# Weight splits queued three halves ahead of their products instead of four

## The chip, the cores and the metric

One core of a Trainium2 chip runs the whole program in one launch. The metric is the device time of that core in microseconds (us), the median of several executions. TensorE multiplies, VectorE and GpSimd do element by element work, ScalarE does functions and casts, and SyncE's queue issues most transfers. In the profile's rows PE is TensorE, PEld its loading of the stationary operand, DVE VectorE, ACT ScalarE, POOL GpSimd, SP SyncE.

## What is computed

One layer with 512 tokens and width 2048, float32. The weights of the modulation, of the two projections and of the feed-forward part are matrices of 2048 rows or columns; every matrix is read once.

```python
mod = silu(c) @ w_ada + b_ada                       # 2048 x 12288, six vectors
sh1, sc1, gt1, sh2, sc2, gt2 = split(mod, 6)
h = rms_norm(x, norm1_g) * (1 + sc1) + sh1
proj = h @ w_in
att = sparse_attention(q, k, v, iq, ik, iw)         # 8 heads, top 128 keys by an index score
rwkv = rwkv7_time_mix(y, ...)                       # 16 heads of 64, a state per head, scanned over tokens
x = x + gt1 * (concat(att, rwkv) @ w_out)
h2 = rms_norm(x, norm2_g) * (1 + sc2) + sh2
ffn = (silu(h2 @ w_gate) * (h2 @ w_up)) @ w_down    # width 5632
out = x + gt2 * ffn
```

## The kernel before

**Products.** Every large product is made of three products of a faster number format, fp32r. A weight tile `wraw` is split into a high part `whi`, a cast on ScalarE, and a low part `wlo` = `wraw` - `whi`, a subtraction on VectorE (or on GpSimd, for odd halves of the middle part of the program). The activations are split alike (`hhi`, `hlo`). TensorE adds `hhi whi`, `hlo whi` and `hhi wlo`. All operations go through one helper, so nearly every row of the profile has its line, L127, and rows are told apart by the names of the tiles.

**The weight stream.** A job is a chunk of weights, mostly 4 k-tiles of 256 columns (512 KB), with the 24 products that use it. `issue_to` loads it into one of three raw buffers. `split_to` splits it in two halves of 512 columns a partition, each with 12 products; there are four buffers for `whi` and four for `wlo`. `run_jobs` writes the stream: at the start of job i it issues the loads up to job i + 2 and splits up to a certain half, and in the middle of the job it splits one half more. `s0` is the number of a job's first half. `split_to(n)` writes the halves below n. Until now the start of a job writes its fourth half counted from `s0` (number `s0 + 3`), the middle writes number `s0 + 4`: each split stands in the queues right behind the products of the half that used its buffer last.

**What sets the order.** The program is written in one pass, and each engine runs its queue in the order in which it was written. Beside the stream, generators write the side work: the preparation of the eight RWKV pairs (`prep`), the scan, the index scores, the attention heads, the sums of the modulation (`ada_stream`, tiles `wad`, added up on GpSimd). `drive` gives each a turn after every three products. A generator goes on when a rough clock for each queue, kept while the program is written, says that its input is there (`until`) or that a queue is not too full (`room`). Splits count in that clock too, so where a split is written moves the side work.

**A preparation** runs from two small products (`pw`) through `sg` (ScalarE, then GpSimd), the scan `L` (VectorE), `kkn`, `kf`, `work` (VectorE) to the transposes `pT` on TensorE, of which the products behind them in TensorE's queue have to wait. `rr` is a reciprocal root of a norm on GpSimd, from `st` on VectorE; `hx`, `hhi`, `hlo` are the activations behind a norm.

**Stages.** Up to about 140 us the first columns of h and the low-rank products; to 600 us the rest of `w_in` beside the preparations; to 1130 us the scan, scores and heads beside the last columns; to 1345 us the out-projection; then norm 2, and gate, up and down in four parts of the width. In the feed-forward part an up-group of two tiles is closed by an evacuation that multiplies and splits on VectorE and ScalarE; there are 22.

Of the kernel before, what the change touches and what calls it, by code (L numbers as in the profile page):

```python
# [14 lines left out]
DRAM = bass.MemoryType.DRAM  # L15
# [25 lines left out]

# columns of the constant table
C_ID, C_MASK, C_CAUS, C_BLKM = 0, 128, 256, 384
# [5 lines left out]
def layer_kernel(ctx, tc, x, c, positions, w_ada, b_ada, norm1_g, w_in, q_norm_g, k_norm_g,  # L49
                 rwkv_mu, rwkv_w0, rwkv_w_up, rwkv_a0, rwkv_a_up, rwkv_g_up, rwkv_k_k, rwkv_k_a,  # L50
                 rwkv_r_k, rwkv_lnx_g, rwkv_lnx_b, w_out, norm2_g, w_ffn_gate, w_ffn_up,
                 w_ffn_down, cst_in, out, dbg=None):
    nc = tc.nc
    ctx.enter_context(tc.manual_schedule())

    # A rough clock for each queue, kept while the program is written: it decides when side work joins the queues.
    clk = dict(pe=0.0, dve=0.0, act=0.0, pool=0.0, dma=0.0)
    ready = {}
    side = {"pe": 0.0}
# [78 lines left out]
    def until(*aps):  # L138
        """let the products run on until what these hold is there."""
        t = max(ready.get(nm(a), 0.0) for a in aps) + SLACK  # L140
        while now() < t:
            yield
# [5 lines left out]
    def banks(n):  # L148
        """wait for n free banks of the side pool."""
        while True:  # L150
            for k in [k for k, v in psread.items() if v is not None and v <= now()]:
                del psread[k]
            if len(psread) + n <= 4 and side["pe"] <= SIDE:
                return
            yield
# [42 lines left out]

    # ---------------------------------------------------------------- constants
    cst = const.tile([128, C_W], F32, name="cst")  # L200
# [27 lines left out]

    # ---------------------------------------------------------------- weight stream
    jobs = []  # L230
# [3 lines left out]
    def job(view, k0, nk, c0, ncols, mms, need=None, before=None, after=None, whole=False):  # L234
        """a chunk of weights, with the products that use it; its two halves are split one by one."""
        j = dict(view=view, k0=k0, nk=nk, c0=c0, n=ncols, mms=mms, need=need, before=before, after=after, i=len(jobs),
                 hi=[], lo=[], s0=len(subs), whole=whole)
        jobs.append(j)
        subs.extend([(j, u) for u in range(min(nk, 2))])
# [25 lines left out]
    def run_jobs(a, b, eng=SP, every=3):  # L265
        for i in range(a, b):
            j = jobs[i]
            while j["need"] is not None and not j["need"]():
                yield
            if j["before"] is not None:  # L270
                j["before"]()
            issue_to(i + 3, eng)
            split_to(j["s0"] + 4)
            n = 0
            half = None
            for kk, o, l, r, st, sp in j["mms"](j):
                if half is None and j["nk"] > 1 and kk >= j["nk"] // 2 and not j["whole"]:
                    half = 1
                    split_to(j["s0"] + 5)
                mm(o, l, r, st, sp)  # L280
                n += 1
                if n % every == 0:
                    yield
            if j["after"] is not None:
                j["after"]()
# [14 lines left out]
    def group_T(view, c0, mts, klist, kc, rhs, evac, pool=PG, need=None, before=None, kneed=None, add=True, chunk_done=None, apart=False):  # L300
        """out^T tiles: mts = [(column offset, M)], contracted over klist in chunks of kc."""
        box = {}
        ncols = mts[-1][0] + mts[-1][1]
        nch = len(klist) // kc

        def mms(j, ci):
            if ci == 0:
                box["ps"] = [pool("acc") for _ in mts]
            order = [(kk, i) for kk in range(kc) for i in range(len(mts))]
            if apart and ci == nch - 1:  # L310
                order.sort(key=lambda e: e[1])
            for kk, i in order:
                ki = ci * kc + kk
                hi, lo = rhs(klist[ki])
                (off, M), ps = mts[i], box["ps"][i]
                wh, wl = j["hi"][kk][:, off:off + M], j["lo"][kk][:, off:off + M]
                yield kk, ps[:M], wh, hi, ki == 0, False
                yield kk, ps[:M], wh, lo, False, False
                yield kk, ps[:M], wl, hi, False, ki == len(klist) - 1
                if apart and ki == len(klist) - 1 and i < len(mts) - 1:  # L320
                    evac(box["ps"], [i])

        def one(ci):
            job(view, klist[ci * kc], kc, c0, ncols, (lambda j, ci=ci: mms(j, ci)),
                need=(kneed(klist[ci * kc:ci * kc + kc]) if kneed else (need if ci == 0 else None)),
                before=before if ci == 0 else None,
                after=(lambda: evac(box["ps"], *([[len(mts) - 1]] if apart else []))) if ci == nch - 1 else chunk_done,
                whole=apart and ci == nch - 1)

        if not add:  # L330
            return one
        for ci in range(nch):
            one(ci)

    # ---------------------------------------------------------------- inputs
    xtok = [[hpool.tile([128, 512], F32, name="xtok", tag="h") for _ in range(4)] for _ in range(NT)]
# [16 lines left out]

    # scale and shift, some columns at a time; the loads run as far ahead as there is room
    BLOCKS = [(0, 1), (1, 1)] + [(k, 2) for k in range(2, KD, 2)]
    pieces = []
    for k1, n1 in BLOCKS:
        for kind in ("scale", "shift"):
            n = 4 // n1
# [34 lines left out]

    # rms of x, and x transposed
    ssq = SM("ssq")
# [12 lines left out]

    # vectors as columns  # L410
    v1 = const.tile([128, 128], F32, name="v1")
# [25 lines left out]
    def tables():  # L437
        """cos and signed sin of the rotary angles, features on partitions."""
        pos = G("pos", I32)
# [4 lines left out]
        for fc, sc in ((C_FQ, C_SQ), (C_FI, C_SI)):  # L444
            ang, n, t = G("ang"), G("nrot"), G("trot")
# [26 lines left out]

    # first group: the loras and two tiles of k, as the columns of h come
    first = []
# [47 lines left out]

    # ---------------------------------------------------------------- modulation, first part
    def colsum(dst, t):
        """column 32 b + c of t, summed over the partitions of a quarter, to partition c of the quarter and column b."""
        u = G("tr")
        V.transpose(u, t)
        V.tensor_reduce(dst, u.rearrange("p (b c) -> p b c", c=32), axis=mybir.AxisListType.X, op=OP.add)

    def spread(ps, parts, col=C_MOD):  # L530
        """the quarters added up: the sum of column 128 j + q to partition q and column j."""
        pv = parts.rearrange("p (j a) -> p a j", a=4)
        for a in range(4):
            mm(ps[32 * a:32 * a + 32], cst[:, col:col + 32], pv[:, a, :])
# [58 lines left out]

    # ---------------------------------------------------------------- rwkv: evacuation with token shift
    def shifted(ps, M, mcol, name):
# [33 lines left out]

    # scratch in DRAM  # L630
    pk = dram.tile([NC, 128, PAIRS, 512], F32, name="pk")
# [143 lines left out]

    # ---------------------------------------------------------------- rwkv: triangular solve, one problem per partition
    solved = set()
# [42 lines left out]

    # ---------------------------------------------------------------- rwkv: chunk scan over all heads
    mix = {}
    scanned = set()

    def scan(g):
        """the pairs of a group, chunk after chunk."""
        while g not in solved or done["prep"] < PAIRS:
# [131 lines left out]

    # ---------------------------------------------------------------- modulation, second part  # L960
    mod = {n: const.tile([128, 16], F32, name=n) for n in ("gt1", "sh2", "sc2", "gt2")}
# [58 lines left out]

    # ---------------------------------------------------------------- attention
    iwt = const.tile([128, NT, 16], F32, name="iwt")
# [142 lines left out]

    # the four query tiles of a head share three banks
    PLACE = {3: (0, 0), 2: (1, 0), 0: (1, 384), 1: (2, 0)}
# [63 lines left out]

    # ---------------------------------------------------------------- the main stream of products
    ALLK = list(range(KD))
# [38 lines left out]

    # out projection, contracted over the rwkv half first
    mT = {}
# [61 lines left out]
    for m in range(4, KD, 2):  # L1336
        group_T(wout, m * 128, TWO, KO, 4, mixed, evac_out(m), kneed=kneed, before=load_x([m, m + 1]),
                apart=m == KD - 2)
    # the column sums of the squares need every tile
    i_norm2 = len(jobs)  # L1340
# [30 lines left out]

    # feed-forward, in parts of its width
    gate = {}
# [48 lines left out]

    # gate and up together in the first group, as the columns of h2 come
    gbox, ubox = {}, {}
# [26 lines left out]

    # ---------------------------------------------------------------- go
    start(run_rb())
# [106 lines left out]
```

## Time and profile before

| | |
|---|---|
| median of 3 runs (lowest to highest) | 2810.62 us (2807.94 to 2813.64) |
| the profiled execution's span | 2808.0 us |
| TensorE busy | 2699.7 us, 96% |
| VectorE, ScalarE, GpSimd busy | 49%, 34%, 29% |
| granted TensorE clock, mean | 0.975 of full |
| the chain that ended last: TensorE, VectorE, DMA | 81%, 9%, 4% |

The span is read by stretches: the share of TensorE's busy time and the granted clock tell which of them can give anything. A wait is shown with the engine that waited, what it waited to write, and what released it. A matmul row may be a few per cent short of records.

### The profile page before, as it was taken

The numbers are of one execution on the slowest core, as the hardware profiler recorded it, in microseconds if no ns is written. First come the engines' busy times: TensorE is split into PE (matmuls) and PEld (weight loads), VectorE is DVE, ScalarE is ACT, GpSimd is POOL, SyncE is SP. The second block draws the span as 40 slices with busy tenths as digits, with TensorE's granted clock in tenths as the row PEclk, the third lists the DMA queues.
The fourth block names the chain that finished last, engine by engine and source line by source line (L and its number), as shares of the span: only waits on it lengthen the run. The fifth ranks groups of instructions, "written<-read, shape, count | busy, mean of one in ns | idle before, by whom it ended". The sixth has DMA issues, their size and how long they took to land.

```text
span 2808.0 us, 35665 instructions
## 1 busy us (share of the span) xinstructions
PE 2699.7 (96%) x13439; PEld 2131.3 (76%) x13439; DVE 1362.6 (49%) x2064; ACT 953.0 (34%) x1691; POOL 801.9 (29%) x695
## 2 busy tenths in 40 slices
PE   7998988988999999999799999999999999999999
PEld 4576766667677768788688888888888888888887
DVE  4476445588957875743743233232333323333333
ACT  3255542332333335554452222222222222222222
POOL 2057768974434566654340000000000000000000
PEclk8999999989999999999899999999999999999999
DMA  9976765355466434464253333323333333333233
GB/s 324 312 243 202 227 184 146 103 131 174 149 198 195 137 128 136 156 220 149 77 193 98 98 98 97 97 95 96 97 98 98 98 98 98 98 98 95 93 101 110
DMA packets 383580, 396.12 MB, mean 141 GB/s; under 512 B 52442, under 2 KB 332832, under 8 KB 383408
## 3 DMA queue, kind: packets, MB, share of 16 engines
q1 hardware_dynamic: 381312, 387.78, 44.5%
q0 software_dynamic: 1952, 5.81, 0.6%
q8 instruction: 105, 1.72, 0.3%
q14 instruction: 67, 0.55, 0.1%
q10 hardware_dynamic: 144, 0.26, 0.0%
HBM read 358.13 MB, written 35.65 MB: 140 GB/s over the span
## 4 chain that ended last, share of the span: by engine, by line
PE 81%; DVE 9%; DMA 4%; POOL 2%; issue 2%; ACT 1%; SPq 1%; DVEq 0%; ACTq 0%; POOLq 0%
PE acc L127 71%; DMA wraw<-in_w_in_dram 2%; PE p L127 1%; DVE X L127 1%; PE po L127 1%; DVE stmp L127 1%; PE vacc L127 1%; DVE work L127 1%; DVE wlo L127 1%; SPq L127 1%; PE adaacc L127 1%; DMA wada<-in_w_ada_dram 1%; DVE score L127 1%; PE pV L127 1%; DVE u L127 0%
## 5 line engine op out<-in xcount | busy, mean ns | idle before, releaser
L127 DVE TENSOR_TENSOR wlo<-wraw,whi 128x512 fp32r<-128x512 f32 (+2 forms) x750 | 553.2, 743 | 1111.3 <-ACT whi L127 1104.8
L127 ACT CAST whi<-wraw 128x512 fp32r<-128x512 f32 (+2 forms) x860 | 517.9, 607 | 1251.9 <-PE acc L127 1085.7
L127 PE MATMUL acc<-hhi,whi 128*128 128x512 f32 (+1 forms) x2256 | 914.4, 405 | 4.4 <-ACT hhi L127 4.0
L127 PE MATMUL acc<-hhi,wlo 128*128 128x512 f32 (+1 forms) x2256 | 887.2, 393 | 19.2 <-DVE wlo L127 15.5
L127 PE MATMUL acc<-hlo,whi 128*128 128x512 f32 (+1 forms) x2256 | 886.2, 393 | 3.6 <-DVE hlo L127 3.6
L127 PEld LDWEIGHTS acc<-hhi,whi 128*128 128x128 f32 (+1 forms) x2256 | 425.2, 188 | 128.4 <-issue 32.4
L127 PEld LDWEIGHTS acc<-hhi,wlo 128*128 128x128 f32 (+1 forms) x2256 | 426.0, 189 | 116.3 <-DVE wlo L127 19.3
L127 PEld LDWEIGHTS acc<-hlo,whi 128*128 128x128 f32 (+1 forms) x2256 | 426.3, 189 | 95.4 <-DVE hlo L127 6.4
L127 PE MATMUL acc<-act,whi 128*128 128x512 f32 x1408 | 434.8, 390 | 0.0
L127 POOL TENSOR_TENSOR wad<-wad 128x512 f32<-128x512 f32 x240 | 343.0, 1429 | 150.5 <-ACT wad L127 139.0
L127 PEld LDWEIGHTS acc<-act,whi 128*128 128x128 f32 x1408 | 263.2, 188 | 53.8
L127 PE MATMUL acc<-act,wlo 128*128 128x512 f32 x704 | 274.0, 389 | 0.0
L127 POOL TENSOR_TENSOR wlo<-wraw,whi 128x512 fp32r<-128x512 f32 (+1 forms) x110 | 157.9, 1436 | 235.4 <-ACT whi L127 223.9
L127 ACT ACTIVATE wad<-wad,cact 128x512 f32<-128x512 f32 x256 | 179.0, 719 | 14.4 <-DMA wad<-in_w_ada_dram 14.1
L127 PEld LDWEIGHTS acc<-act,wlo 128*128 128x128 f32 x704 | 132.1, 188 | 27.6
L127 PE MATMUL acc<-mhi,whi 128*128 128x512 f32 x256 | 100.5, 392 | 0.0
L127 PE MATMUL acc<-mhi,wlo 128*128 128x512 f32 x256 | 99.7, 389 | 0.0
L127 PE MATMUL acc<-mlo,whi 128*128 128x512 f32 x256 | 99.6, 389 | 0.0
L127 DVE SCALAR_TENSOR_TENSOR x<-acc,gt,x 128x512 f32<-128x512 f32 x80 | 57.3, 750 | 41.6 <-PE acc L127 41.6
L127 POOL TENSOR_TENSOR X<-X,stmp 128x504 f32<-128x504 f32 (+33 forms) x69 | 67.0, 970 | 5.4
L127 POOL TENSOR_TENSOR stmp<-X,N 128x504 f32<-128x504 f32 (+33 forms) x69 | 63.7, 923 | 4.6 <-DVE work L127 1.4
L127 PE MATMUL vacc<-whi,hhi 128*128 128x512 f32 x128 | 58.1, 454 | 0.0
(257 smaller groups left out, 2328.5 us busy)
## 6 DMA issues: line engine op xcount, KB each, us to landing
wad<-in_w_ada_dram SPq DMA_DIRECT2D x256, 256.0 KB, 4.4
wraw<-in_w_in_dram SPq DMA_DIRECT2D x108, 512.0 KB, 5.0
wraw<-in_w_ffn_down_dram SPq DMA_DIRECT2D x88, 512.0 KB, 3.4
wraw<-in_w_ffn_gate_dram SPq DMA_DIRECT2D x84, 512.0 KB, 3.5
wraw<-in_w_ffn_up_dram SPq DMA_DIRECT2D x84, 512.0 KB, 3.4
wada<-in_w_ada_dram SPq DMA_DIRECT2D x128, 256.0 KB, 6.7
wraw<-in_w_out_dram SPq DMA_DIRECT2D x32, 512.0 KB, 3.5
pk<-pack SPq DMA_DIRECT2D x16, 768.0 KB, 3.8
```

The costliest lines, as they stand in the source:

```text
L127: return f(*args, **kw)
```

## The change

The two calls of `split_to` in `run_jobs` ask for one half less. At the start of a job the half `s0 + 2` is written, in its middle the half `s0 + 3`. Buffers and loads stay as they are in number and size. All other lines of the diff take away comments and docstrings, and are left out here.

```diff
@@ -270,13 +270,13 @@
             if j["before"] is not None:
                 j["before"]()
             issue_to(i + 3, eng)
-            split_to(j["s0"] + 4)
+            split_to(j["s0"] + 3)
             n = 0
             half = None
             for kk, o, l, r, st, sp in j["mms"](j):
                 if half is None and j["nk"] > 1 and kk >= j["nk"] // 2 and not j["whole"]:
                     half = 1
-                    split_to(j["s0"] + 5)
+                    split_to(j["s0"] + 4)
                 mm(o, l, r, st, sp)
```

VectorE's queue in the second preparation, before; `tr` and `part` belong to a sum of the modulation:

```order
L127 SCALAR_TENSOR_TENSOR L<-reset,sg 128x512
L127 SCALAR_TENSOR_TENSOR kkn<-k,v_231,prb 128x512
L127 TENSOR_SCALAR kf<-at,v_231,der 128x512
L127 TENSOR_TENSOR kf<-k,kf 128x512
L127 SCALAR_TENSOR_TENSOR work<-kkn,sg 128x8x63
L127 TENSOR_SCALAR work<-kkn 128x8
L127 TENSOR_TENSOR work<-r,sg 128x8x64
L127 TENSOR_TENSOR wlo<-wraw,whi 128x512
L127 STREAM_TRANSPOSE tr<-wad 128x512
L127 TENSOR_REDUCE part_377<-tr 128x16
L127 TENSOR_TENSOR at<-at,e_2471 128x512
L127 TENSOR_TENSOR work<-kkn,at 128x8x64
```

and the same place now:

```order
L127 SCALAR_TENSOR_TENSOR L<-reset,sg 128x512
L127 SCALAR_TENSOR_TENSOR kkn<-k,v_231,prb 128x512
L127 TENSOR_SCALAR kf<-at,v_231,der 128x512
L127 TENSOR_TENSOR kf<-k,kf 128x512
L127 SCALAR_TENSOR_TENSOR work<-kkn,sg 128x8x63
L127 TENSOR_SCALAR work<-kkn 128x8
L127 TENSOR_TENSOR work<-r,sg 128x8x64
L127 TENSOR_TENSOR at<-at,e_2484 128x512
L127 TENSOR_TENSOR work<-kkn,at 128x8x64
L127 TENSOR_TENSOR work<-kf,e_2484 128x8x64
L127 SCALAR_TENSOR_TENSOR r<-r,v_231,kf 128x512
L127 TENSOR_TENSOR wlo<-wraw,whi 128x512
```

The low part that stood between `work` and `at` has moved behind `r`, and the small sum has gone ahead of `L`.

GpSimd's queue where the heads end and the out-projection is about to begin, before:

```order
L127 TENSOR_TENSOR wad<-wad 128x512 x2
L127 TENSOR_TENSOR rr<-st,cst 128x4
L127 TENSOR_SCALAR rr<-rr 128x4
L127 TENSOR_TENSOR wad<-wad 128x512
L127 TENSOR_TENSOR rr<-st,cst 128x4
L127 TENSOR_SCALAR rr<-rr 128x4
L127 TENSOR_TENSOR wlo<-wraw,whi 128x512
L127 TENSOR_TENSOR wad<-wad 128x512
```

and now:

```order
L127 TENSOR_TENSOR wlo<-wraw,whi 128x512
L127 TENSOR_TENSOR wad<-wad 128x512 x2
L127 TENSOR_TENSOR rr<-st,cst 128x4
L127 TENSOR_SCALAR rr<-rr 128x4
L127 TENSOR_TENSOR rr<-st,cst 128x4
L127 TENSOR_SCALAR rr<-rr 128x4
L127 TENSOR_TENSOR wlo<-wraw,whi 128x512
L127 TENSOR_TENSOR wad<-wad 128x512 x2
```

The two pairs of `rr` stood ahead of one low part and `wad` additions; now they stand behind fewer additions and ahead of the low part that comes one job earlier in the stream.

VectorE's queue at the start of the feed-forward part, with the numbers of the tiles, before:

```order
L127 TENSOR_TENSOR hlo_11683<-hx_11680,hhi_11682 128x512
L127 TENSOR_TENSOR wlo_11692<-wraw_11621,whi_11691 128x256
L127 TENSOR_TENSOR wlo_11696<-wraw_11621,whi_11695 128x256
L127 TENSOR_SCALAR hx_11701<-hx_11701,gp2_376,sh2_373 128x512
L127 TENSOR_TENSOR hlo_11704<-hx_11701,hhi_11703 128x512
L127 TENSOR_SCALAR hx_11708<-hx_11708,gp2_376,sh2_373 128x512
L127 TENSOR_TENSOR hlo_11711<-hx_11708,hhi_11710 128x512
L127 TENSOR_SCALAR hx_11721<-hx_11721,gp2_376,sh2_373 128x512
L127 TENSOR_TENSOR hlo_11724<-hx_11721,hhi_11723 128x512
L127 TENSOR_TENSOR wlo_11729<-wraw_11689,whi_11728 128x256
L127 TENSOR_TENSOR wlo_11741<-wraw_11689,whi_11740 128x256
```

and now:

```order
L127 TENSOR_TENSOR hlo_11773<-hx_11770,hhi_11772 128x512
L127 TENSOR_TENSOR wlo_11782<-wraw_11677,whi_11781 128x256
L127 TENSOR_TENSOR wlo_11786<-wraw_11711,whi_11785 128x256
L127 TENSOR_SCALAR hx_11791<-hx_11791,gp2_376,sh2_373 128x512
L127 TENSOR_TENSOR hlo_11794<-hx_11791,hhi_11793 128x512
L127 TENSOR_SCALAR hx_11798<-hx_11798,gp2_376,sh2_373 128x512
L127 TENSOR_TENSOR hlo_11801<-hx_11798,hhi_11800 128x512
L127 TENSOR_SCALAR hx_11811<-hx_11811,gp2_376,sh2_373 128x512
L127 TENSOR_TENSOR hlo_11814<-hx_11811,hhi_11813 128x512
L127 TENSOR_TENSOR wlo_11819<-wraw_11711,whi_11818 128x256
L127 TENSOR_TENSOR wlo_11831<-wraw_11779,whi_11830 128x256
```

Each low part has moved back by one place in the row of low parts: of the two that stand between `hlo` and the next `hx`, the first is now the second half of the chunk before (`wraw_11677` is the chunk that `wraw_11587` was), and the second half of the next chunk (`wraw_11711`, which was `wraw_11621`) stands behind the three `hx` and `hlo`.

## Rows read from the trace of the kernel before

**Rows 1.** By stretch: length, PE, PEld, DVE, ACT, POOL busy (instructions), clock, DMA share, GB/s.

```profile
300.00:400.00 100.00, 89.15 (x463) 68.82 (x462) 53.41 (x60) 45.59 (x77) 72.35 (x55) 0.93 0.72 208
1400.00:1800.00 400.00, 400.00 (x1772) 330.97 (x1771) 138.42 (x197) 123.90 (x204) 34.03 (x26) 1.00 0.35 113
```

**Rows 2.** Waits of all engines between 140 and 460 us; engine, line, releaser: total, times, longest.

```profile
POOL wlo L127 <- ACT whi L127: 88.8, 21, 25.7
...
DVE wlo L127 <- ACT whi L127: 88.0, 23, 11.8
...
ACT whi L127 <- DMA wraw<-in_w_in_dram: 60.1, 12, 8.8
...
ACT whi L127 <- PE acc L127: 26.7, 18, 4.6
...
PE pT L127 <- DVE work L127: 23.6, 5, 5.9
```

**Rows 3.** Waits between 460 and 800 us.

```profile
PE pT L127 <- DVE work L127: 12.6, 2, 7.1
...
PE acc L127 <- DVE wlo L127: 7.1, 3, 3.7
```

**Rows 4.** Waits between 1420 and 2808 us, the feed-forward part.

```profile
ACT whi L127 <- PE acc L127: 872.2, 435, 2.6
```

**Rows 5.** Timeline of VectorE and GpSimd, preparations; start, length, operation, [idle before, releaser].

```profile
211.73 0.63 POOL L127 TENSOR_SCALAR sg<-sg 128x512 f32<-128x512 f32 x1
...
212.86 1.63 DVE L127 TENSOR_TENSOR_SCAN L<-reset,sg 128x512 f32<-128x512 f32 x1
...
250.11 0.69 DVE L127 TENSOR_TENSOR wlo<-wraw,whi 128x512 fp32r<-128x512 f32 x1 [7.91 <-ACT whi L127]
...
257.33 1.77 DVE L127 TENSOR_TENSOR wlo<-wraw,whi 128x512 fp32r<-128x512 f32 x1
...
260.36 1.76 DVE L127 TENSOR_TENSOR at<-at,e 128x512 f32<-128x512 f32 x1
...
451.88 0.62 POOL L127 TENSOR_SCALAR sg<-sg 128x512 f32<-128x512 f32 x1
...
456.75 2.07 DVE L127 TENSOR_TENSOR_SCAN L<-reset,sg 128x512 f32<-128x512 f32 x1
```

**Rows 6.** Stretches behind two of the waits at pT; columns as in the first group.

```profile
226.00:232.00 6.00, 5.86 (x36) 4.49 (x36) 5.56 (x7) 3.96 (x7) 5.87 (x4) 0.74 0.75 236
573.00:579.00 6.00, 6.00 (x33) 4.47 (x31) 5.44 (x7) 0.76 (x2) 5.76 (x6) 0.64 0.08 26
```

**Rows 7.** Instruction groups: VectorE 140-460 us, VectorE 1420-2808 us, GpSimd 140-460 us; count, busy, mean ns.

```profile
L127 DVE TENSOR_TENSOR wlo<-wraw,whi 128x512 fp32r<-128x512 f32 x42 | 43.1, 1033 | 87.0 <-ACT whi L127 86.5
...
L127 DVE TENSOR_TENSOR wlo<-wraw,whi 128x512 fp32r<-128x512 f32 x502 | 347.3, 695 | 839.2 <-ACT whi L127 836.5 <-PE fin L127 2.5
...
L127 POOL TENSOR_TENSOR wad<-wad 128x512 f32<-128x512 f32 x77 | 113.1, 1469 | 11.8 <-ACT wad L127 8.4
```

**Rows 8.** Timeline around 1140 us: GpSimd, then TensorE.

```profile
1132.96 6.89 POOL L127 TENSOR_TENSOR rr<-st,cst 128x4 f32<-128x4 f32 x1 [6.02 <-DVE st L127]
...
1143.40 1.59 POOL L127 TENSOR_TENSOR wlo<-wraw,whi 128x512 fp32r<-128x512 f32 x1
...
1145.04 0.50 PE L127 MATMUL acc<-hhi,wlo 128*128 128x512 f32 x1 [2.87 <-POOL wlo L127]
```

**Rows 9.** Timeline at the start of the feed-forward part: VectorE, then TensorE.

```profile
1360.25 5.73 DVE L127 TENSOR_TENSOR wlo<-wraw,whi 128x256 fp32r<-128x256 f32 x4
...
1361.78 0.80 PE L127 MATMUL acc<-hhi,wlo 128*128 128x512 f32 x1 [7.06 <-DVE wlo L127]
```

**Rows 10.** Timeline of VectorE behind an up-evacuation.

```profile
1619.55 0.69 DVE L127 TENSOR_TENSOR gate<-acc,gate 128x512 f32<-128x512 f32 x1 [0.92 <-PE acc L127]
...
1623.52 1.28 DVE L127 TENSOR_TENSOR wlo<-wraw,whi 128x512 fp32r<-128x512 f32 x2
```

**Rows 11.** The page's costliest groups: the first products.

```profile
L127 PE MATMUL acc<-hhi,whi 128*128 128x512 f32 (+1 forms) x2256 | 914.4, 405 | 4.4 <-ACT hhi L127 4.0
```

## The prediction

> **What bounds the kernel now.** I read the table by stretches first. From 1400 us on TensorE is busy all the time at the full granted clock: 1772 matmuls in 400 us, so 0.226 us for one and 2.71 us for the 12 products of a half [rows 1]. No edit can shorten that stretch except by removing products, and this one removes none. In front of it TensorE is idle for most of the 108 us that its busy total lacks to the span, for instance 11 us between 300 and 400 us, where the clock also stands at 0.93 [rows 1]. So the question is which wait ends last there.
>
> The waits of 140 to 460 us answer it [rows 2]. TensorE's own large wait is at pT, the transposes that close a RWKV preparation: 23.6 us in 5, released by VectorE's work, and another 12.6 us in 2 up to 800 us [rows 3]. That is 36.2 us in seven. After each the granted clock falls: six windows of 5 to 7 us behind such a wait have 0.74 in the first and 0.64 in the last [rows 6], with 0.70, 0.76, 0.59 and 0.64 between. The missing share times the length is 11.8 us, or about 2.0 us for one.
>
> The other large waits of that stretch are where the split sits [rows 2]: ScalarE at whi, for a buffer that TensorE still reads (26.7 us) or for the load (60.1 us), and behind ScalarE the low parts on VectorE (88.0 us) and GpSimd (88.8 us). These cost nothing by themselves. They cost when a step of the preparation stands behind one in the same queue. The scans L show it [rows 5]: the factor sg, made by GpSimd, is there at 211.73 + 0.63 = 212.36, and L starts at 212.86, 0.5 us later; the last of the six that stand behind a low part has sg at 452.50 and starts at 456.75, 4.2 us later. Over the six (0.5, 3.6, 1.1, 2.7, 0, 4.2) that is 12.1 us. For the second, the low part ahead of L starts at 250.11 after 7.91 us of waiting for whi [rows 5].
>
> **What the split itself costs when it moves.** No split is added or removed. One that is queued a half later has a buffer that has been free for a half, so ScalarE no longer stops there for TensorE. Its lead until use falls from three halves to two, 8.13 to 5.42 us. SyncE's load that reuses the raw buffer is released one half later too, and so is everything behind it in SyncE's queue.
>
> In the feed-forward part I cost this at nothing: ScalarE waits there 872.2 us for TensorE, in 435 waits [rows 4], so cast and subtraction have slack. The cover is thinnest behind an up-evacuation: VectorE multiplies from 1619.55, and its next low parts start at 1623.52 [rows 10]. The first of them ends about 1624.2, and with a lead of two halves from the evacuation it is due at 1619.5 + 5.42 = 1624.9. So 0.7 us are left, before there were 3.4. If that cover went by 0.3 us, it would cost 22 times 0.3 = 6.6 us.
>
> **Preparations.** Three terms. (1) L is freed: between 0 and 12.1 us [rows 5]; I take 12.1, since the low part in front of it no longer waits for TensorE. (2) The writer's clock, freed of those waits too, places pT earlier: counted in the two orders, the products between a preparation's first matmul and its pT fall in the eight from 78, 78, 99, 72, 102, 81, 102, 72 to 75, 66, 87, 72, 81, 84, 96, 66, by 57, and 57 x 0.226 = 12.9 us of cover are lost. (3) What stands inside the chain: the second loses a low part and two small ones, from 257.33 to 260.36, 3.0 us, the fourth one such low part of 1.77, and the first and the third gain one each of 1.77 [rows 5]: -1.3. Together -12.1 + 12.9 - 1.3 = -0.5 us, and as the number of waits stays, the clock stays as it is. Ends: -19 us, if each of seven waits shrank by a half of 2.71, and +12.9, if only term 2 came.
>
> **Additions of the ada stream.** GpSimd gets ten more wad additions up to about 400 us (87 in place of 77 in its order), at 1.469 us each [rows 7]. They delay VectorE, whose low parts take 1.033 us there and 0.695 in the feed-forward part [rows 7]: 0.34 us lost on each, beside 77 additions and 40 low parts of GpSimd. Ten more in 117 raise that by 0.03 us per operation; with some 12 such operations in a chain and eight chains it is 2.8 us, and I take +2, with ends of 0 and 10 x 1.469 = 14.7 us.
>
> The Trainium skill (SBUF — State Buffer, "Who interferes with whom") says that a VectorE instruction with two SBUF inputs and a GpSimd instruction that reads SBUF exclude each other, and that the loser blocks fully for the other's whole instruction. The measured mean agrees that they hinder each other, but its 0.34 us shows that most meet only in part; by the rule's worst case this term alone would be the 14.7.
>
> **600 to 700 us.** TensorE waits here three times for VectorE's low parts, 7.1 us [rows 3]. In the new order six scoring operations stand later, and VectorE has less between these low parts; against that the lead is shorter by 2.71 us. I take -3, ends -7.1 and +14 (three waits that grow by 2.71 and 2.0 of clock each).
>
> **Heads, before the out-projection.** On GpSimd four small rr now stand ahead of the low part of a half whose use comes 24 products earlier. Before, the first rr waited 6.02 us for VectorE's st and took until 1139.85, the low part started at 1143.40, and TensorE waited 2.87 us for it [rows 8]. If rr stays where it is, TensorE meets it 24 x 0.226 = 5.4 us earlier; if st comes earlier by as much, nothing changes. With nothing to decide, the middle: +2.7.
>
> **Start of the feed-forward part.** Four low parts of 1.43 us stand behind the making of h2 and start at 1360.25; TensorE waits 7.06 us for them [rows 9]. Now one more low part, used six products earlier than the first of those four, has moved behind the three h2 rows and leads them. VectorE's work ahead of it is nearly the same, so TensorE stops 6 x 0.226 = 1.4 us earlier and goes on at the same time: +1.4 (at the lower clock level, 1.2 GHz, twice that).
>
> **Up to 140 us.** hhi now stands ahead of a whi on ScalarE; all such waits of the kernel are 4.0 us [rows 11]. I take -1, ends -4 and 0.
>
> **Sum**: -0.5 + 2 - 3 + 2.7 + 1.4 - 1 = +1.6 us. Against the profiled execution, 2808.0 + 1.6 = 2809.6 us; the median of the runs shown is 2.6 above that execution, so 2812.2 us.
>
> **Rivals.**
> (a) The shorter lead decides. Place: the three waits at low parts between 600 and 700 us [rows 3]. Price: 2.71 us and 2.0 us of clock at each. From one place, 1.6 + 3 + 4.7 = +9.3, 2820 us, to all three, 1.6 + 3 + 14 = +18.6, 2829 us. It decides where VectorE's queue holds more than 5.42 us of work ahead of a low part. For it: VectorE is the late one there already. Against: the new order has less work at that spot. Chance 0.28.
> (b) The freed queues win. Not only L but all steps ahead of it on VectorE and GpSimd come earlier, as 88 us of waiting on either go [rows 2], and the waits at pT shrink by a half each: four of them give 1.6 - 10.8 = -9.2, 2801 us, all seven 1.6 - 19.0 = -17.4, 2793 us. Against: the pT were placed earlier as well, and 60.1 us of ScalarE's waiting is for loads [rows 2], which come no sooner. Chance 0.27.
> (c) GpSimd's ten additions hold VectorE at full length each, 14.7 in place of 2: +14.3, 2825 us. The 0.34 us above speaks against it. Chance 0.03. This is the case that the Trainium skill's page would give.
> (d) The edit does little, because loads and the four buffers set the same times: 2810.6 us. Against it: the order shows some thousand rows that moved. Chance 0.05.
>
> **How the numbers follow.** A measurement of this kernel can tell about 0.2%, 5.6 us, from no change. The forecast has 0.37, of which 0.02 spill over on either side. Same is 0.33 + 0.05 = 0.38; faster is 0.27 + 0.02 = 0.29; slower is 0.28 + 0.03 + 0.02 = 0.33. The range leaves out a tenth on either side, the outer third of (a) and of (b) with what lies beyond: 2796 to 2830 us. The forecast's own range is 2805 to 2818.
>
> **What would show it.** In the changed profile ScalarE's waits at whi for TensorE between 140 and 460 us should nearly vanish and VectorE's at wlo shrink; L should start at most 0.7 us after sg; seven to eight waits at pT should remain, with a sum within 6 us of 36.2 and the clock falling as before. A sum under 25 us is (b). More or longer waits of TensorE at wlo between 600 and 700 us or at the heads are (a). In the feed-forward part any wait at wlo behind an up-evacuation would make the zero wrong, by 22 times its length. The forecast is wrong as a whole if the writer's order, which I only compared at these places, makes a new wait where none was.

## The result and the profile after

The changed kernel takes 2834.06 us (median of 4, 2829.82 to 2837.05), the kernel before 2809.95 us on the same chip: a ratio of 1.0088, 95% interval 1.0076 to 1.0101. That is 24 us slower. The forecast of 2812 with a range to 2830 was wrong.

The profiled execution has a span of 2835.3 us, 27.3 more than before. To see where they lie, I counted TensorE's 10032 weight products in either trace, which stand in the same order in both, and took the time from the start of one to the start of a later one; the first stretch begins with TensorE's first instruction and the last ends with its last. "Idle" is TensorE's own idle time in the stretch; the rest is matmuls, at either clock level. Times in us.

| products | what it is | before | after | difference | idle before, after | my term |
|---|---|---|---|---|---|---|
| to 576 | first columns, low-rank products, rotary tables | 211.5 | 228.9 | +17.4 | 18.3, 29.2 | -1 |
| 576 to 1600 | preparations | 383.8 | 383.1 | -0.7 | 46.0, 45.5 | -0.5 + 2 |
| 1600 to 3100 | scan, scores, heads, first out-projection | 595.7 | 606.0 | +10.3 | 24.9, 28.5 | -3 + 2.7 |
| 3100 to 3696 | out-projection | 143.4 | 142.8 | -0.6 | 5.4, 5.4 | 0 |
| 3696 to 3900 | norm 2, first gate and up | 61.6 | 63.0 | +1.4 | 8.8, 9.3 | +1.4 |
| from 3900 | feed-forward | 1398.8 | 1398.8 | 0.0 | 0.5, 0.5 | 0 |

So the feed-forward part lost nothing, as forecast, and most of the loss lies in the 220 us to which I had given -1.

TensorE's longest groups of waits over the whole changed kernel (engine, what it wanted to write, releaser: total, times, longest):

```profile
PE pT L127 <- DVE work L127: 27.7, 8, 6.1
PE acc L127 <- DVE wlo L127: 18.3, 10, 7.3
PE acc L127 <- ACT whi L127: 12.8, 8, 2.8
...
PE acc L127 <- POOL wlo L127: 5.7, 8, 1.6
```

The same groups before, with one wait at pT that another engine released:

```profile
PE pT L127 <- DVE work L127: 36.2, 7, 7.1
PE acc L127 <- DVE wlo L127: 15.5, 6, 7.1
...
PE acc L127 <- POOL wlo L127: 3.6, 3, 2.9
PE pT L127 <- ACT rl L127: 3.2, 1, 3.2
...
PE acc L127 <- ACT whi L127: 0.5, 2, 0.2
```

Three things are to be seen. The waits at pT have fallen from 39.4 us in eight, 36.2 in the seven of [rows 2, 3] and 3.2 in one more, to 27.7 in eight. The waits for low parts on VectorE have grown; of these 7.3 are one wait at the start of the feed-forward part, as before [rows 9]. And a group is there that hardly existed: waits at whi, 12.8 us in 8, where the trace of before has 0.5 in 2.

Three places make 12.1 us of the 17.4 that are lost before product 576. The first, ScalarE and then TensorE (start, length, operation, idle before and its releaser):

```profile
86.61 0.82 ACT L127 ACTIVATE hhi<-hx,sh,gp 128x512 fp32r<-128x512 f32 x1 [4.24 <-DVE hx L127]
89.37 0.81 ACT L127 ACTIVATE hhi<-hx,sh,gp 128x512 fp32r<-128x512 f32 x1 [1.95 <-DVE hx L127]
90.09 1.32 ACT L127 CAST whi<-wraw 128x448 fp32r<-128x448 f32 x3
...
90.69 0.48 PE L127 MATMUL acc<-hhi,whi 128*96 128x512 f32 x1 [1.33 <-ACT whi L127]
...
92.08 0.47 PE L127 MATMUL acc<-hhi,wlo 128*96 128x512 f32 x1 [0.68 <-DVE wlo L127]
```

The cast stands in ScalarE's queue behind two `hhi`, and these wait for VectorE's `hx`, which waits for products of the modulation. TensorE is there before the cast. The granted clock of 92 to 96 us is 0.60, between its two levels of 1.2 and 2.4 GHz. By product 120 the changed kernel is 3.7 us further behind than at product 108. Not all of that is the wait: 16 more products of the modulation stand in this stretch now, which cost 1.1 us in e2, where nothing waits.

The second place, the evacuation of the low-rank products, a chain that goes to and fro between ScalarE and VectorE:

```profile
155.93 0.68 ACT L127 ACTIVATE xw<-acc,der 96x512 f32<-96x512 f32 x1 [1.34 <-PE acc L127]
157.42 0.63 ACT L127 ACTIVATE xw<-xw 96x512 f32<-96x512 f32 x1 [0.81 <-DVE xw L127]
...
162.12 0.63 ACT L127 ACTIVATE xg<-xg 128x512 f32<-128x512 f32 x1 [0.82 <-DVE xg L127]
...
162.66 1.12 ACT L127 CAST whi<-wraw 128x512 fp32r<-128x512 f32 x2
...
163.31 0.50 PE L127 MATMUL acc<-hhi,whi 128*128 128x512 f32 x1 [2.62 <-ACT whi L127]
```

The chain holds ScalarE from 155.93 to 162.66, 6.7 us. A lead of two halves is 5.4 us [rows 1]. Before, the cast for this half stood ahead of the chain, at 146.30; now it stands behind it. ScalarE before:

```profile
146.30 0.62 ACT L127 CAST whi<-wraw 128x512 fp32r<-128x512 f32 x1 [0.63 <-ACT whi L127]
147.19 0.69 ACT L127 ACTIVATE xw<-acc,der 96x512 f32<-96x512 f32 x1 [0.27 <-PE acc L127]
```

The wait is 2.62 us, with a granted clock of 0.66 from 163 to 168 us: 4.3 us in all between products 276 and 312.

The third place, the rotary tables:

```profile
187.89 0.61 ACT L127 CAST whi<-wraw 128x512 fp32r<-128x512 f32 x1
196.59 0.63 ACT L127 ACTIVATE nrot<-nrot 128x512 f32<-128x512 f32 x1 [8.09 <-DVE nrot L127]
197.13 0.61 ACT L127 ACTIVATE ang<-ang 128x512 f32<-128x512 f32 x1
197.65 0.60 ACT L127 CAST whi<-wraw 128x512 fp32r<-128x512 f32 x1
...
194.62 0.50 PE L127 MATMUL acc<-hhi,wlo 128*128 128x512 f32 x1 [1.46 <-DVE wlo L127]
...
198.30 0.50 PE L127 MATMUL acc<-hhi,whi 128*128 128x512 f32 x1 [1.09 <-ACT whi L127]
```

ScalarE stands 8.09 us at a sine that waits for VectorE's range reduction, and the next cast stands behind the sine. Here 4.1 us are lost between products 408 and 432.

The other 5.3 us lie ahead of product 108 (1.4) and between products 120 and 276 (3.9). Of the latter e2, below, has 2.5 and e1 0.3, so they come mostly with the new order; what makes them is open.

### The profile page after: what moved, and what is told of

Same layout as the page of the kernel before. It is cut to its first block, busy times and chain, and to the rows that moved or that the text cites. A ratio compares the mean times of both kernels' runs of the same rounds, so it can differ in the third digit from the quotient of the medians.

```text
span 2835.3 us, 35513 instructions
## 1 busy us (share of the span) xinstructions
PE 2712.8 (96%) x13439; PEld 2135.7 (75%) x13439; DVE 1362.2 (48%) x2064; ACT 940.7 (33%) x1691; POOL 792.6 (28%) x695
## 4 chain that ended last, share of the span: by engine, by line
PE 69%; DVE 6%; issue 1%; ACT 1%; POOL 0%; DMA 0%; DVEq 0%; ACTq 0%; POOLq 0%
PE acc L127 62%; PE vacc L127 2%; PE p L127 2%; PE po L127 2%; DVE X L127 1%; DVE stmp L127 1%; DVE wlo L127 1%; PE pl L127 1%; DVE score L127 0%; DVE u L127 0%; PE pgt L127 0%; PE pt L127 0%; PE pst L127 0%; PE dot L127 0%; PE prb L127 0%
## 5 line engine op out<-in xcount | busy, mean ns | idle before, releaser
L127 PE MATMUL acc<-hhi,whi 128*128 128x512 f32 (+1 forms) x2256 | 916.5, 406 | 17.0 <-ACT whi L127 12.8
L127 PE MATMUL acc<-hhi,wlo 128*128 128x512 f32 (+1 forms) x2256 | 891.4, 395 | 24.1 <-DVE wlo L127 18.3
L127 ACT CAST whi<-wraw 128x512 fp32r<-128x512 f32 (+2 forms) x860 | 511.3, 606 | 965.6 <-PE acc L127 896.6
L127 ACT CAST act<-gate 128x512 fp32r<-128x512 f32 x44 | 27.3, 621 | 138.8 <-DVE gate L127 138.8
L127 DVE TENSOR_TENSOR gate<-acc,gate 128x512 f32<-128x512 f32 x44 | 30.2, 687 | 76.4 <-PE acc L127 76.4
```

The lines of the kernel that those rows point to most:

```text
L127: return f(*args, **kw)
```

## Experiments

Two theories of the loss. **Lead**: a split one half later stands behind more side work in its queues, and TensorE comes to its half first. **Order**: the split is charged to the writer's rough clock one half later, so the side work is written elsewhere among the products, and it is that order that costs. A third, **luck**, came up on the way: any small change of that clock deals the side work anew, and this was one bad deal.

### Lead and order apart

The rough clock and the instructions can be separated. `plan_to` charges the clock for a split, `split_to` writes its two instructions and charges nothing. e1 writes late and charges early, e2 the reverse:

```diff
-            split_to(j["s0"] + 4)
+            plan_to(j["s0"] + 4)       # e1; e2 has 3 here, behind the split
+            split_to(j["s0"] + 3)      # e1; e2 has 4 here
...
-                    split_to(j["s0"] + 5)
+                    plan_to(j["s0"] + 5)       # e1; e2 has 4 here, behind the split
+                    split_to(j["s0"] + 4)      # e1; e2 has 5 here
```

The splits get two helper lines of their own by that, L288 and L289 in rows. In the traces the operations of ScalarE, VectorE and GpSimd other than splits stand in e1 in the order of the kernel before, and in e2 in that of the changed kernel.

> The splits are written one half later, as in the changed kernel, but the writer's rough clock is charged for them where it was before, so that all side work keeps the place among TensorE's products that it had before. Lead theory (a split one half later stands behind more side work in ScalarE's and VectorE's queues, and TensorE reaches its half first): most of the loss of 25 us stays, +15 to +25 against before, with waits at whi and wlo before 200 us. Order theory (the loss comes from side work that was written elsewhere): within 3 us of before.

Measured: 2805.99 against 2808.97 us, ratio 0.9992 (0.9982 to 1.0002), no difference that can be told.

> The reverse: the splits are written where they were before, but the writer's rough clock is charged for them one half later, so that the side work stands among TensorE's products as in the changed kernel. Lead theory: the loss is gone, -8 to +8 against before. Order theory: +20 to +28.

Measured: 2840.43 against 2808.97 us, ratio 1.0114 (1.0099 to 1.0129), 31 us slower, more than either theory had.

The lead theory, which I held before these runs, falls: the shorter lead alone costs nothing on the whole, and the new order alone costs more than the edit. By stretches, against before:

| products | edit | e1, late, old order | e2, early, new order |
|---|---|---|---|
| to 576 | +17.4 | +4.8 | +6.7 |
| 576 to 1600 | -0.7 | -9.1 | +8.0 |
| 1600 to 3100 | +10.3 | +1.0 | +17.6 |
| 3100 to 3696 | -0.6 | -0.2 | -0.6 |
| 3696 to 3900 | +1.4 | +1.4 | 0.0 |
| from 3900 | 0.0 | 0.0 | 0.0 |

Among the preparations the two act against each other, and their sum, -1.1, is about the edit's -0.7. To product 576 they do not add up: 4.8 and 6.7 make 11.5, together they cost 17.4. By places: the first needs both, for neither e1 nor e2 has a wait there. The second is lead alone: e1 has the wait at product 289 with 2.64 us and loses 3.9 by product 312, e2 has none. The third is order alone: e2 waits there for 3.00 us in spite of the long lead, e1 does not wait. The start of the feed-forward part is lead alone.

### The place

The edit in a part of the jobs only:

```diff
-            split_to(j["s0"] + 4)
+            late = 1 if i < nfirst + 12 else 0      # e3; e4: i >= nfirst + 12
+            split_to(j["s0"] + 4 - late)
...
-                    split_to(j["s0"] + 5)
+                    split_to(j["s0"] + 5 - late)
```

> The edit only in the first 30 jobs (the first 576 products, until about 220 us); all later splits as before. If the place of the loss is the first 200 us, as the difference of the two traces by product suggests (+17 there): +14 to +22 against before. If the loss is spread over the whole front part: +3 to +10.

Measured: 2822.75 against 2808.97 us, ratio 1.0055 (1.0039 to 1.0070), +14 us; in its trace it is +13.7 to product 576 and -4 behind it.

> The edit only from the 31st job on; the first 30 as before. If the place of the loss is the first 200 us: +3 to +10 against before, and the feed-forward part adds at most 2. If spread: +15 to +22.

Measured: 2807.18 against 2808.97 us, ratio 0.9996 (0.9987 to 1.0006), less than the +3 to +10 expected. The place is the first 220 us: with the splits there as before, nothing of the loss is left, although the side work behind product 576 was dealt anew in e4 as well. But the two parts, +14 and -2, make 12 of the edit's 24: from 1600 to 3100 e3 has -1.3 and e4 +4.0, where the edit has +10.3.

e6 asks what of these first jobs is lead. It has the order of the changed kernel throughout and gives only the first 30 jobs their long lead back:

```diff
+            late = 1 if i >= nfirst + 12 else 0
+            plan_to(j["s0"] + 3)
-            split_to(j["s0"] + 3)
+            split_to(j["s0"] + 4 - late)
...
-                    split_to(j["s0"] + 4)
+                    split_to(j["s0"] + 5 - late)
+                    plan_to(j["s0"] + 4)
```

> Side work in the order of the changed kernel throughout; the splits of the first 30 jobs are written where they were before, all later ones a half later, as changed. If the loss before product 576 (17 us in the changed kernel) needs both the shorter lead and the new order: about 6 us are left of it (as in e2), and the whole stands at +14 to +19 against before. If the new order alone made it: +22 to +28.

Measured: 2824.89 against 2808.69 us, ratio 1.0056 (1.0042 to 1.0070), +16 us. To product 576 it is +6.4 in place of +17.4, and the first two places are without a wait. TensorE's only wait from 152 to 222 us in e6:

```profile
PE acc L127 <- ACT whi L288: 3.0, 1, 3.0
```

It is the third place, and there the long lead does not help. ScalarE in e2, where it looks the same:

```profile
176.14 0.61 ACT L288 CAST whi<-wraw 128x512 fp32r<-128x512 f32 x1
187.28 0.63 ACT L127 ACTIVATE nrot<-nrot 128x512 f32<-128x512 f32 x1 [10.52 <-DVE nrot L127]
187.81 0.61 ACT L127 ACTIVATE ang<-ang 128x512 f32<-128x512 f32 x1
188.33 0.60 ACT L288 CAST whi<-wraw 128x512 fp32r<-128x512 f32 x1
...
188.99 0.50 PE L127 MATMUL acc<-hhi,whi 128*128 128x512 f32 x1 [3.00 <-ACT whi L288]
```

### The tables

That the third wait comes from the sine's place was so far read from the timeline. e13 (from e6) and e14 (from the changed kernel) take the tables away from there:

```diff
-    start(tables())
+    def tables_later():
+        while state["split"] < jobs[nfirst + 15]["s0"]:
+            yield
+        yield from tables()
+
+    start(tables_later())
```

> e6 (order of the changed kernel, first 30 splits where they were) with the rotary tables begun 15 jobs later, so that their sines stand behind the casts of the products 288 to 576. If the 6 us that e2 and e6 lose between products 288 and 576 come from a cast that stands behind a sine which waits for VectorE: those products take 68.5 us as before, without a wait at whi. If something else makes it: 73 to 75 us as in e6. What lies behind product 576 is dealt anew and says nothing.

> The changed kernel with the rotary tables begun 15 jobs later. Products 288 to 576: the waits at about 195 us go, the one at product 289 behind the evacuation of the low-rank products stays with 2.6 us and its clock; 71 to 73 us in place of 74.1. If the tables are not the cause of the waits at 195 us: 74 us.

One execution each: 2815.51 us for e13 and 2833.68 for e14, the kernel before 2815.04. In the stretch that I had named both miss the expected time, 78.1 and 82.7 us: the first pT, with its wait, now falls inside of it. The waits themselves answer. In e13 TensorE has none from 152 to 222 us, and at product 552 it is 0.4 us ahead of before, where e6 was 6.6 behind. In e14 the wait at product 289 is there with 2.64 us and those at 195 us are gone; at product 528 it is 11.3 us behind, and all of it was there at product 312. So the tables are the cause at the third place. Whether moving them is worth anything, one execution each can't say: e13 stands level with the kernel before beside it, where e6 was 16 us slower, and its trace is 6.8 us ahead of e6's at product 1600; e14 is 19 us slower than before and at product 1600 no further ahead than the changed kernel.

### Luck

To see how touchy the time is, I changed only the margin that the writer adds before side work may follow its input, in the kernel before and in the changed one:

```diff
-    SLACK = 0.5
+    SLACK = 0.4      # e7, e9; e8, e10: 0.6; e11: 1.0
```

> The kernel before, only the margin that the writer adds before it lets side work follow its input is 0.4 in place of 0.5 us. Splits stay four halves ahead. If the time depends on where side work falls by small differences of the writer's clock, whatever causes them, this moves the time by 5 us or more, either way. If the loss needs the split's move, it stays within 3 us of before.

> As e7 with a margin of 0.6 us: moves by 5 us or more, either way, if the order of the side work is touchy; within 3 us if not.

> The changed kernel with the writer's margin at 0.4 in place of 0.5 us. Systematic theory (a split that is charged to the writer's clock later makes that clock too early everywhere, and the loss belongs to the edit): 2825 us or more, at or above the changed kernel's 2834 since less margin places side work earlier still. Luck theory (the edit only dealt the side work anew, and this deal was a bad one): anywhere within 10 us of 2810.

> The changed kernel with the margin at 0.6 us. Systematic theory: between 2820 and 2834 us, a little less than the changed kernel, as e8 was less than the kernel before. Luck theory: within 10 us of 2810.

> The kernel before with twice the margin, 1.0 us. If the trend of e7 and e8 (0.4: 2820, 0.5: 2809, 0.6: 2801) is one, that is, if the writer's clock is too early and later side work is better: 2785 to 2800 us. If e7 and e8 were two draws: anywhere from 2800 to 2822.

| margin, us | kernel before | ratio (interval) | changed kernel | ratio (interval) |
|---|---|---|---|---|
| 0.4 | 2820.02 (e7) | 1.0043 (1.0028 to 1.0059) | 2832.37 (e9) | 1.0085 (1.0070 to 1.0100) |
| 0.5 | 2809.95 | 1 | 2834.06 | 1.0088 (1.0076 to 1.0101) |
| 0.6 | 2801.20 (e8) | 0.9973 (0.9962 to 0.9985) | 2836.87 (e10) | 1.0106 (1.0089 to 1.0123) |
| 1.0 | 2828.94 (e11) | 1.0077 (1.0062 to 1.0092) | | |

The ratios are taken against the kernel before with 0.5 beside the same run. A tenth of a microsecond in a planning constant moves the kernel before by 8 to 11 us. The time is not a trend of it: at 1.0 it is 2829, outside of both expectations, so my reading of e7 and e8 as "later side work is better" falls; e10 also came out above its range. The edit costs something at each margin tried, but from about 12 us at 0.4 to 37 at 0.6. By stretches:

| products | before, margins 0.4, 0.5, 0.6, 1.0 | changed, margins 0.4, 0.5, 0.6 |
|---|---|---|
| to 576 | 212.4, 211.5, 213.5, 214.8 | 235.8, 228.9, 227.5 |
| 576 to 1600 | 379.8, 383.8, 377.0, 381.5 | 377.1, 383.1, 380.6 |
| 1600 to 3100 | 609.3, 595.7, 592.2, 616.9 | 600.2, 606.0, 605.7 |
| 3696 to 3900 | 61.6, 61.6, 61.7, 61.6 | 63.3, 63.0, 63.0 |

To product 576 the two kernels stand apart at every margin tried, by 12.6 us at the least; so does the start of the feed-forward part, by 1.3 to 1.7. Those losses belong to the edit. From 1600 to 3100 the changed kernel's times lie inside the 25 us over which the margin alone throws the kernel before. The +10.3 there can't be told from luck, and I leave it open which of its waits belongs to the edit.

### A faster version

In e1 the late splits gain from product 576 to 2100 (-9.1 up to 1600 and -8.3 from there) and lose elsewhere (+9.3 from 2100 to 3100), with the side work in its old order. e5 does only that: `plan_to` as in e1, `late = 1 if nfirst + 12 <= i < nfirst + 75 else 0`, and `split_to` with 4 - late and 5 - late.

> All side work keeps its old place, and only the splits of jobs 31 to 93 (products 576 to 2100) are written a half later. By the segments of e1: 0 before product 576, -9 from 576 to 1600, -8 from 1600 to 2100, 0 behind it: about -17 against before (-8 to -20), faster than both kernels. If e1's gain in the middle needed its later start, or was luck of one execution: within 4 us of before.

Measured: 2792.41 against 2808.69 us, ratio 0.9937 (0.9925 to 0.9950), 16 us faster than before and, by the two ratios, 42 faster than the changed kernel. Against before it has +1.3 to product 576, -11.5 to 1600, -8.0 to 2100. The waits at pT, the first row, are what fell; low parts on GpSimd, the last, are what grew, from 3.6 us in 3:

```profile
PE pT L127 <- DVE work L127: 24.6, 7, 4.4
PE acc L127 <- DVE wlo L289: 13.4, 3, 7.0
PE acc L127 <- POOL wlo L289: 11.6, 6, 4.0
```

e12 is e5 with e8's margin of 0.6:

> e5 (splits of jobs 31 to 93 a half later, side work as the clock of the kernel before places it) with the margin of e8. If the two gains add up, 17 and 8 us: 2782 to 2788 us. If e5's gain needs that one order of the side work: 2795 to 2802.

Measured: 2798.76 against 2807.92 us, ratio 0.9969 (0.9957 to 0.9982), about e8's 0.9973. The two gains do not add up: what e5 gains in one order of the side work is not there in e8's.

## Why the prediction was wrong

**The feed-forward part: right.** From product 3900 on the time is the same to the tenth, 1398.8 us. The thin place behind the up-evacuation held.

**Its start: right in size.** +1.4 forecast, +1.4 measured; e1 has it and e2 not, so it is the lead, as the six products said. In the changed kernel, VectorE and then TensorE:

```profile
1386.43 5.73 DVE L127 TENSOR_TENSOR wlo<-wraw,whi 128x256 fp32r<-128x256 f32 x4
...
1387.96 0.79 PE L127 MATMUL acc<-hhi,wlo 128*128 128x512 f32 x1 [7.32 <-DVE wlo L127]
```

TensorE waits 7.32 us in place of 7.06 [rows 9], and at the product six places earlier.

**The preparations: the sum right, its terms not.** -0.5 forecast, and +2 for the additions; -0.7 measured. What the additions cost alone was not tried. The signs were right: freed queues gain (e1, -9.1, where I had -12.1 - 1.3), earlier side work loses (e2, +8.0, where I had +12.9; the products between a preparation's first matmul and its pT are in e2 and in the changed kernel the ones that I had counted). In the new order the lead gains nearly as much, 8.7 us from e2 to the changed kernel. But the mechanism of term 1 was wrong. L was to start at once after sg. In the second preparation of the changed kernel, ScalarE and then VectorE:

```profile
269.95 0.62 ACT L127 CAST whi<-wraw 128x512 fp32r<-128x512 f32 x1 [3.94 <-DMA wraw<-in_w_in_dram]
...
270.61 1.75 DVE L127 TENSOR_TENSOR wlo<-wraw,whi 128x512 fp32r<-128x512 f32 x1 [7.63 <-ACT whi L127]
272.29 1.21 DVE L127 TENSOR_TENSOR_SCAN L<-reset,sg 128x512 f32<-128x512 f32 x1
```

A low part still stands ahead of L and waits 7.63 us, now because the load isn't there. I had taken the wait for the buffer as the one that ends last; the 60.1 us of waiting for loads stood in the same rows [rows 2]. Over the same six preparations L starts 11.0 us after sg, before 12.1, and over all eight 29.9, before 22.4. What did fall most is the way ahead of L, which only rival (b) had named: from a preparation's first small product to the end of sg, over eight, from 101.0 to 85.6 us, and in e1, with the old order, to 94.1; with the new order and the old lead (e2) it is 100.1. The way from L to the last work fell from 104.6 to 98.3, but it is 109.6 in e1, so it doesn't carry the lead's gain. Of the checks that I named, ScalarE's waits for TensorE between 140 and 460 us fell from 26.7 to 11.8 us and did not nearly vanish, and those for loads, which I had held fixed, fell from 60.1 to 24.7:

```profile
ACT whi L127 <- DMA wraw<-in_w_in_dram: 24.7, 7, 6.8
...
ACT whi L127 <- PE acc L127: 11.8, 7, 2.6
```

And a sum of pT waits within 6 us of 36.2 failed: it is 27.7. My seven also left out the eighth, with its 3.2 us. Part of what the pT waits gave back went to waits at whi and wlo between the preparations, 2.3 us before and 12.0 now from product 576 to 1600, so that the stretch stayed as long.

**Up to 140 us: the step that failed.** I bounded it by the waits for `hhi`, 4.0 us in the whole kernel [rows 11], with a gain as the only sign, and stopped at 140 us. That row shows what TensorE waits for now; it can't show a wait that the change makes. The queue to look at was ScalarE's: what stands ahead of a split there that itself waits for another engine, and for how long. Three such stood there (two `hhi` behind `hx`; the evacuation with 6.7 us; the sines with 8.1 us), two of them longer than the new lead of 5.4; in the new order the sines outlast the old lead of 8.1 too (e2, 10.52 us). The last two stand between 140 and 220 us, for which I had no term. The working had that number and had applied it to VectorE's queue between 600 and 700 us alone. Measured: +17.4 for -1, with 12.1 at these places: the first needs lead and order together, the second is the lead, the third the order (e1 +4.8, e2 +6.7 in all).

**600 to 700 us and the heads: the stretch is not to be judged.** -3 + 2.7 forecast, +10.3 measured from 1600 to 3100. The margin alone moves this stretch by 25 us, so a sum by hand to 3 us had no ground there. The lead itself was worth +1.0 in e1. The two waits that I had priced can be looked at: between 600 and 700 us one at a low part with 3.6 us and one at whi with 0.7 are left of 7.1, near the -3; at the heads the 2.87 us are gone, in e2 too, where I had +2.7. Neither makes the +10.3.

**The rivals.** (a), a lead shorter than the work ahead of a split, was the right mechanism for the three places before product 576, about half of the loss, but not where I had put it. (b) was right about the preparations: the late split gives 9.1 us there in the old order and 8.7 in the new one. In the edit the new order takes 8.0 of that back; e5 keeps the old one and has the gain.

## What to carry to other kernels

Where a program is ordered by a planner's clock, an edit has two parts, what it does on the chip and what it does to the plan. Write the instruction and the charge apart and run all four combinations; here one part alone made no difference on the whole and the other alone cost 31 us. And before an order is judged by one timing, move a constant of the planner by a hair: the scatter that this gives, here 28 us, is the least that a difference from a new order has to exceed in its stretch.

When a lead is cut, go through the queue of each engine that the split uses, from the first instruction of the program on, and look for work that waits for another engine for longer than the new lead.

## What the runs showed that I had not expected

A planning margin of 0.4, 0.5, 0.6 and 1.0 us gives 2820, 2810, 2801 and 2829 us in the same kernel. Short waits of TensorE can cost more than they last: the 2.62 us at product 289 made 4.3 by product 312, with a granted clock of 0.66 from 163 to 168 us, and in e2 3.00 us at product 433 made 5.2 by product 456, with 0.73 from 188 to 192 and 0.92 from 192 to 200 us. Not each does: the two waits of the first place, 1.33 and 0.68 us, are in e3 as well, with 1.33 and 0.69, and there the granted clock stays at 1.00 from 86 to 98 us.

The range reduction ahead of the sine, the longest of the three chains, is slowed by GpSimd. Two steps of one kind, VectorE and beside it GpSimd, in the changed kernel:

```profile
182.29 1.41 DVE L127 TENSOR_SCALAR nrot<-ang 128x512 f32<-128x512 f32 x1
...
194.49 0.42 DVE L127 TENSOR_SCALAR nrot<-ang 128x512 f32<-128x512 f32 x1
...
181.93 1.48 POOL L127 TENSOR_TENSOR wad<-wad 128x512 f32<-128x512 f32 x1
```

At 194.49 GpSimd stands idle and the step takes 0.42 us, at 182.29 it adds up `wad` and a step of the same kind takes 1.41. So it is a chain's length beside GpSimd that has to be set against a lead. The Trainium skill (SBUF — State Buffer, "Who interferes with whom") counts such an operation among those that can take the port pair shared with GpSimd and so block and be blocked; the trace agrees that it is held, by 0.99 us of the 1.48 that the addition takes.
